# Expert pairs of a two-block decoder kernel: scatter and gather queued behind the next bias product

## The chip, the cores and the metric

One NeuronCore of one Trainium2 chip runs the whole program. The metric is the device time of one execution in microseconds, as the median of several executions of the same program. All tensors are float32, and the weights come from HBM.

## The reference, cut to what matters

The first block mixes tokens (gated delta rule and gated linear attention) and ends in a mixture of experts; the second block has two dense decoder layers with attention. The change lies in the experts alone:

```python
def moe_ffn(h, w_router, b_router, w_gu, b_gu, w_down, b_down):
    # h: 256 tokens x 1024; 32 experts, each token goes to its 4 best
    logits = h @ w_router + b_router
    top_logit, top_idx = lax.top_k(logits, 4)
    top_p = softmax(top_logit)
    # for every expert e, with the tokens that chose it (rows xb):
    gu = xb @ w_gu[e] + b_gu[e]                 # 1024 -> 2048: gate and linear half
    act = clamped_swiglu(gu)                    # sigmoid(1.702 g) * g * (l + 1), clamped at 7
    y = act @ w_down[e] + b_down[e]             # 1024 -> 1024
    # out[token] += p(token, e) * y
```

Every expert's weights are read once: 8 MB for gate and linear half, 4 MB for the way down, 12 MB for each of 32 experts (402.7 MB in all).

## The kernel before, in words

**Tiling.** `moe` keeps 64 rows for each expert (CAP) and works on two experts at a time, so that a pair fills the 128 columns of TensorE: 16 pairs, n = 0 to 15. Two pairs make a block (b = 0 to 7). Per block, a *gather* builds one-hot matrices S (VectorE, L1326) and multiplies the tokens by them (L1337: 8 feature tiles of 4 products each into a `tr` buffer), and `scaled` brings each tile to SBUF, on VectorE (L1245) and ScalarE (L1243) in turn, as `xg` (odd blocks) or in the resident `resB` (even blocks). So `xg` has two places, and the gather of the next block overwrites nothing that the current one reads.

**One pair.** (1) Gate and linear products: 8 steps kk, each with two 1 MB weight tiles, into the PSUM tiles `gt` and `lt` (L1354), closed by the bias products (L1358). (2) `swiglu`: VectorE clamps `gt` and `lt` (L1251, L1252), ScalarE does three passes (L1253 to L1255), VectorE two products (L1256, L1257). (3) `act_T`: 8 transposes (L1264) through two `tr` buffers, copied by ScalarE (L1265). (4) Way down: 4 steps f2, two 1 MB tiles each, into `yd` (L1374). (5) `scatter`: two transposes of the routing weights `sp` (L1272), a ScalarE copy to `spT` (L1274), `ys` = `yd` x gain on VectorE (L1278), and for each of 2 x 2 quarters a product with `spT` into a `tr` buffer (L1281) that VectorE adds to the residual `x1`, which is `resA` in the trace (L1282).

**Buffers.** `gt`, `lt` and `yd` have one buffer each and fill six of the eight PSUM banks. The other two are the two `tr` buffers, which the gather, the scatter, `act_T`, the bias sums and the setup of the second block all share. In SBUF, `ys` has two buffers, used in turn by `ys` itself and by ScalarE's `sg`.

**Weights.** `Experts` holds a ring of 14 tiles of 1 MB and issues every load on SyncE's queue (L1103) in the order of use. A load is issued when the ring slot that it overwrites has been read. Seventeen tiles are under way before the first pair begins.

**What sets the order.** The program is traced in Python order. The framework's scheduler then writes each engine's queue: at every point it takes the earliest traced instruction whose inputs and buffers its own plan holds to be ready. The engines run their queues strictly in order. After block 3 stands `overflow` (L1293): a branch for experts with over 64 rows, over which no instruction is moved; each engine's queue comes to it on its own. After pair 15 comes the second block, whose weights take the ring's place.

The order of tracing inside a block is plain:

```python
for b in range(8):
    S, xg = ...                        # gather of block b
    for pr in range(2):
        ...                            # gate and linear products, bias products
        swiglu(gt, lt, act)
        aT = act_T(act)
        ...                            # way down into yd
        scatter(sp, yd, squares if e0 == 30 else None)
```

Of the kernel before, what the change touches and what calls it, by code (L numbers as in the profile page):

```python
# [9 lines left out]
F32 = mybir.dt.float32  # L10
# [3 lines left out]
ALU = mybir.AluOpType  # L14
# [1114 lines left out]
CAP = 64  # L1129


def moe(k, weights, A, B):
# [132 lines left out]
            nc.scalar.copy(aT[:, 4 * q:4 * q + 4, :].rearrange("p f s -> p (f s)"), pt)  # L1265
        return aT

    def scatter(sp, yd, fn=None):

        pt = tr(256)  # L1270
        for t in range(2):
            nc.tensor.transpose(pt[:, t * 128:(t + 1) * 128], sp[:, t, :], ident)  # L1272
        spT = wk.tile([128, 256], F32, name=k.nm("spT"), tag="spT", bufs=1)
        nc.scalar.copy(spT, pt)  # L1274
        ys = wk.tile([128, 1024], F32, name=k.nm("ys"), tag="ys", bufs=2)
        for j in range(2):
            js = slice(j * 512, j * 512 + 512)
            nc.vector.tensor_mul(ys[:, js], yd[:, js], g2r[:, js])  # L1278
            for t in range(2):
                o = tr()  # L1280
                nc.tensor.matmul(o, spT[:, t * 128:(t + 1) * 128], ys[:, js], start=True, stop=True)  # L1281
                nc.vector.tensor_add(x1[:, t, js], x1[:, t, js], o)  # L1282
                if fn is not None:
                    fn(t, j)
# [6 lines left out]
    def overflow():  # L1291
        mx = nc.values_load(cnt[0:1, 32:33], min_val=0, max_val=256)
        with tc.If(mx > CAP):  # L1293
            for blk in range(2):
                lo = CAP + 128 * blk
                with tc.For_i(0, 32, 1) as e:
                    ce = nc.values_load(cnt[0:1, bass.ds(e, 1)], min_val=0, max_val=256)
                    with tc.If(ce > lo):
                        big_expert(k, L, e, lo)
            nc.vector.memset(flag, 0.0)  # L1300
        p = one.tile([128, 2, 32], F32, name="posm")
        nc.vector.tensor_scalar_add(p, pos, flag)
        return p
# [13 lines left out]
        nc.scalar.activation(jk, x1[:, t, j * 512:j * 512 + 512], AF.Square, accum_out=s4[:, t, j:j + 1])  # L1317

    iota = k.iota[:, 0:CAP]
    for b in range(8):  # L1320
        if b == 4:
            posm = overflow()
        S = []
        for t in range(2):
            s = wk.tile([128, 4, CAP], F32R, name=k.nm("S"), tag="S", bufs=4)
# [7 lines left out]
        for f in range(8):  # L1333
# [3 lines left out]
                    nc.tensor.matmul(o, hx[:, t, f * 128:(f + 1) * 128], S[t].rearrange("p e s -> p (e s)"),  # L1337
                                     start=(t == 0 and i == 0), stop=(t == 1 and i == 1))
            scaled(xg[:, f, :], o, f)
        for pr in range(2):  # L1340
            e0 = 4 * b + 2 * pr
            sp = wk.tile([128, 2, 128], F32, name=k.nm("sp"), tag="sp", bufs=2)
            for t in range(2):
                nc.vector.tensor_tensor(sp[:, t, :].rearrange("p (e s) -> p e s", e=2), S[t][:, 2 * pr:2 * pr + 2, :].bitcast(F32),
                                        prob[:, t, e0:e0 + 2].unsqueeze(2).to_broadcast([128, 2, CAP]), op=ALU.mult)
            gt = ps.tile([128, 1024], F32, name=k.nm("gt"), tag="gt", bufs=1)
            lt = ps.tile([128, 1024], F32, name=k.nm("lt"), tag="lt", bufs=1)
            quarter = lambda j: (gt, gt, lt, lt)[j][:, (j % 2) * 512:(j % 2) * 512 + 512]
            for kk in range(8):
                w = weights.two()  # L1350
                for j in range(4):
                    for i in range(2):
                        c0 = (2 * pr + i) * CAP
                        nc.tensor.matmul(quarter(j)[64 * i:64 * i + 64], xg[:, kk, c0:c0 + CAP],  # L1354
                                         w[i][:, j * 512:(j + 1) * 512], start=(kk == 0), stop=False)
            for j in range(4):
                for i in range(2):
                    nc.tensor.matmul(quarter(j)[64 * i:64 * i + 64], ident[:, 32 * j + e0 + i:32 * j + e0 + i + 1].to_broadcast([128, 64]),  # L1358
                                     bgu, start=False, stop=True)
            if e0 == 0:  # L1360
                early.__exit__(None, None, None)
                wk.late = P("mlate", reuse_waits="tile")
            if e0 == 12:
                biases(weights_T())
            act = wk.tile([128, 1024], F32, name=k.nm("act"), tag="act", bufs=1)
            swiglu(gt, lt, act)
            aT = act_T(act)
            yd = ps.tile([128, 1024], F32, name=k.nm("yd"), tag="yd", bufs=1)
            for f2 in range(4):
                w = weights.two()  # L1370
                for f in range(2):
                    for j in range(2):
                        for i in range(2):
                            nc.tensor.matmul(yd[64 * i:64 * i + 64, j * 512:(j + 1) * 512],  # L1374
                                             aT[:, 2 * f2 + f, 64 * i:64 * i + 64], w[i][:, f, j * 512:(j + 1) * 512],
                                             start=(f2 == 0 and f == 0), stop=(f2 == 3 and f == 1))
            scatter(sp, yd, squares if e0 == 30 else None)
            if e0 in (18, 22, 26):
                q = next(setup)

    s2 = one.tile([128, 2], F32, name="ms2")
    r2 = one.tile([128, 2], F32, name="mr2")
# [10 lines left out]
def big_expert(k, L, e, lo):  # L1393
# [46 lines left out]
    for f in range(8):  # L1440
        w = wk.tile([128, 1024], F32, name=k.nm("bew"), tag="ys", bufs=2)
        nc.sync.dma_start(w, w_dn[bass.ds(e, 1), f * 128:(f + 1) * 128, :].rearrange("o p d -> p (o d)"))
        for j in range(2):
            nc.tensor.matmul(yd[:, j * 512:(j + 1) * 512], aT[:, f, :], w[:, j * 512:(j + 1) * 512],
                             start=(f == 0), stop=(f == 7))
    L["scatter"](sp, yd)


def phase2_setup(k, one, tmp, psum):
# [620 lines left out]
```

## Time and profile before

| | |
|---|---|
| median of 3 executions | 2501.57 us (2495.52 to 2501.66) |
| the profiled execution's own time | 2501.63 us |
| its span, first to last instruction | 2499.9 us |
| mean granted TensorE clock | 0.958 of full |
| TensorE busy (matmuls) | 2288.2 us, 92% of the span |
| VectorE, ScalarE, GpSimdE busy | 1252.3, 929.0, 151.1 us |
| read from HBM | 602.3 MB, 241 GB/s over the span |

The expert stage lies between about 740 and 1740 us of the span. A busy TensorE is not TensorE at its peak: matmuls overlap, and each row's time includes the pipeline. In a row of a timeline the brackets at the end hold the idle time of the engine before the instruction and what ended it. Times are microseconds from the start of the span.

### The profile page before, as it was taken

Reading aid. Unit: us, or ns where it says so; the run is one execution under the profiler, and the core shown is the slowest. Engines: PE = TensorE matmul, PEld = TensorE weight load, DVE = VectorE, ACT = ScalarE, POOL = GpSimd, SP = SyncE. Lnnn points to the kernel's source line nnn. Section 1 sums busy time; section 2 is a strip of 40 time slices with the busy share of each in tenths; the row PEclk is TensorE's granted clock in tenths of the full one; section 3 lists DMA queues with packets and bytes.
Section 4 is the critical chain, followed back from the end, with each engine's and each line's share of the span. In section 5 each row is a group of like instructions: output and inputs, shape, how many; then the busy total and the mean of one; then the engine's idle time right before and its main releaser. Section 6 shows DMA issues by size and latency. Waiting matters only on the chain.

```text
span 2499.9 us, 36297 instructions
## 1 busy us (share of the span) xinstructions
PE 2288.2 (92%) x14402; PEld 1517.2 (61%) x14403; DVE 1252.3 (50%) x2676; ACT 929.0 (37%) x1956; POOL 151.1 (6%) x186
## 2 busy tenths in 40 slices
PE   6689878999989999999899999998999999999998
PEld 3476557889973333333333333333887999887998
DVE  4998887687561111112211121112867656866655
ACT  4556545577430101010001010102466555465545
POOL 0122122000010000000000000000011000011001
PEclk8799988999989999999999999999999999999999
DMA  8532331234988999999999999996534555534553
GB/s 284 139 85 55 114 112 35 60 87 117 284 304 350 407 412 401 417 404 398 387 373 415 414 413 401 407 400 230 158 105 138 175 178 159 154 111 132 189 181 109
DMA packets 290347, 605.87 MB, mean 242 GB/s; under 512 B 26038, under 2 KB 218681, under 8 KB 254332
## 3 DMA queue, kind: packets, MB, share of 16 engines
q1 hardware_dynamic: 283236, 595.24, 64.8%
q10 hardware_dynamic: 6280, 7.80, 1.2%
q8 instruction: 115, 1.88, 0.3%
q0 software_dynamic: 656, 0.46, 0.1%
q14 instruction: 60, 0.49, 0.1%
HBM read 602.30 MB, written 1.15 MB: 241 GB/s over the span
## 4 chain that ended last, share of the span: by engine, by line
PE 42%; DVE 4%; ACT 2%; issue 2%; POOL 0%; ACTq 0%; DVEq 0%; POOLq 0%
PE qm L164 22%; PE yd L1374 5%; PE gt L1354 4%; PE lt L1354 4%; PE tr L1281 1%; PE qm L1781 1%; DVE wl L151 1%; PE tr L1337 1%; PE gt L1358 0%; PE tr L1264 0%; DVE u L1587 0%; DVE act L1257 0%; DVE g L1251 0%; DVE ul L151 0%; ACT sg L1255 0%
## 5 line engine op out<-in xcount | busy, mean ns | idle before, releaser
L150 ACT CAST wh<-w 128x1024 fp32r<-128x1024 f32 (+2 forms) x318 | 318.5, 1002 | 282.6 <-PE qm L164 201.3
L151 DVE TENSOR_TENSOR wl<-w,wh 128x1024 fp32r<-128x1024 f32 (+2 forms) x318 | 372.2, 1171 | 38.9 <-ACT wh L150 37.0
L164 PE MATMUL qm<-uh,wh 128*128 128x272 f32 (+2 forms) x1008 | 260.6, 293 | 0.6 <-ACT wh L150 0.5
L1374 PE MATMUL yd<-w,aT 128*64 128x512 f32 x1024 | 260.0, 639 | 0.6 <-ACT aT L1265 0.4
L164 PE MATMUL qm<-ul,wh 128*128 128x272 f32 (+2 forms) x1008 | 257.4, 289 | 1.3 <-DVE ul L151 1.3
L1251 DVE TENSOR_SCALAR g<-gt 128x1024 f32<-128x1024 f32 x16 | 19.6, 1225 | 409.4 <-PE gt L1358 353.9
L1253 ACT ACTIVATE sg<-g 128x1024 f32<-128x1024 f32 x16 | 16.9, 1056 | 538.5 <-DVE g L1251 538.5
L164 PEld LDWEIGHTS qm<-uh,wh 128*128 128x128 f32 (+1 forms) x1008 | 188.4, 187 | 10.3 <-issue 5.8
L164 PEld LDWEIGHTS qm<-ul,wh 128*128 128x128 f32 (+1 forms) x1008 | 189.1, 188 | 3.5 <-DVE ul L151 1.9
L1354 PE MATMUL gt<-w,resB 128*64 128x512 f32 x512 | 184.0, 598 | 0.0
L1354 PE MATMUL lt<-w,resB 128*64 128x512 f32 x512 | 181.3, 593 | 0.6 <-DVE act L1252 0.6
L1354 PE MATMUL gt<-w,xg 128*64 128x512 f32 x512 | 178.3, 595 | 0.0
L1354 PE MATMUL lt<-w,xg 128*64 128x512 f32 x512 | 177.5, 593 | 0.0
L1374 PEld LDWEIGHTS yd<-w,aT 128*64 128x64 f32 x1024 | 79.0, 148 | 162.0 <-issue 153.6
L164 PE MATMUL qm<-uh,wl 128*128 128x272 f32 (+2 forms) x1008 | 144.7, 285 | 0.0
L164 PE MATMUL mm<-hTh,wh 128*128 128x256 f32 (+1 forms) x384 | 130.9, 360 | 9.6 <-ACT wh L150 4.1
L164 PEld LDWEIGHTS qm<-uh,wl 128*128 128x128 f32 (+1 forms) x1008 | 131.8, 187 | 0.5 <-issue 0.4
L164 PE MATMUL qm<-fl,wh 128*128 128x272 f32 (+1 forms) x512 | 128.5, 286 | 0.0
L164 PE MATMUL qm<-fh,wh 128*128 128x272 f32 (+1 forms) x512 | 127.3, 286 | 0.0
L164 PE MATMUL mm<-hTl,wh 128*128 128x256 f32 (+1 forms) x384 | 126.8, 349 | 0.0
L1354 PEld LDWEIGHTS lt<-w,resB 128*64 128x64 f32 x512 | 53.6, 137 | 73.0 <-issue 71.2
L1354 PEld LDWEIGHTS lt<-w,xg 128*64 128x64 f32 x512 | 53.4, 137 | 71.8 <-issue 71.4
(586 smaller groups left out, 4302.2 us busy)
## 6 DMA issues: line engine op xcount, KB each, us to landing
w<-in_w_gu_dram SPq DMA_DIRECT2D x256, 1024.0 KB
w<-in_w_down_dram SPq DMA_DIRECT2D x128, 1024.0 KB
w<-in_w_ff_dram SPq DMA_DIRECT2D x64, 1024.0 KB
w<-in_w_in_dram SPq DMA_DIRECT2D x72, 512.0 KB
w<-in_w_in_dram SPq DMA_DIRECT2D x30, 1024.0 KB
y<-in_w_mod_dram SPq DMA_DIRECT2D x19, 1024.0 KB
w<-in_w_out_dram SPq DMA_DIRECT2D x24, 512.0 KB
w<-in_w_mod_dram SPq DMA_DIRECT2D x5, 1024.0 KB
```

The lines of the kernel that those rows point to most:

```text
L150: k.nc.scalar.copy(hi, x)
L151: k.nc.vector.tensor_sub(lo, x, hi.bitcast(F32))
L164: mm = nc.tensor.matmul(out, l, r, start=start and n == 1, stop=stop and n == 3 * len(terms))
L1251: nc.vector.tensor_scalar(g, gt, 7.0, LOW / 1.702, op0=ALU.min, op1=ALU.max)
L1253: nc.scalar.activation(sg, g, AF.Exp, scale=-1.702)
L1281: nc.tensor.matmul(o, spT[:, t * 128:(t + 1) * 128], ys[:, js], start=True, stop=True)
L1337: nc.tensor.matmul(o, hx[:, t, f * 128:(f + 1) * 128], S[t].rearrange("p e s -> p (e s)"), start=(t == 0 and i == 0), stop=(t == 1 and i = ...
L1354: nc.tensor.matmul(quarter(j)[64 * i:64 * i + 64], xg[:, kk, c0:c0 + CAP], w[i][:, j * 512:(j + 1) * 512], start=(kk == 0), stop=False)
L1374: nc.tensor.matmul(yd[64 * i:64 * i + 64, j * 512:(j + 1) * 512], aT[:, 2 * f2 + f, 64 * i:64 * i + 64], w[i][:, f, j * 512:(j + 1) * 512] ...
L1781: nc.tensor.matmul(o[r, f:], v[:n, j, r], keys(ts[i], j, n)[:, f - KQ[j]:], start=(j == 0), stop=(j == 2))
```

## The change

The gather, the gate and linear products and the way down become functions, and the two loops become one over 16 pairs. `scatter` is split: `taken` (the product of `yd` with the gain, into `ys`) stays right behind a pair's way down, and the rest, with the transposes of `sp`, the products with `spT` and the sums into `x1`, is traced in the next pair, behind its `swiglu`. There the gather of the next block is traced too (after the odd pairs but 7 and 15), and in pair 6 the bias sums. All TensorE instructions of that stretch get an edge to the pair's last bias product `mm`: in TensorE's queue they come behind it, without a wait on it. Pair 7's scatter is traced ahead of the overflow branch, the gathers of blocks 0 and 4 stay ahead of their pairs, and pair 15's scatter comes after the loop. (`big_expert`, in the branch, calls both halves one after the other.)

```diff
@@ -1265,17 +1265,23 @@
             nc.scalar.copy(aT[:, 4 * q:4 * q + 4, :].rearrange("p f s -> p (f s)"), pt)
         return aT
 
-    def scatter(sp, yd, fn=None):
+    def taken(yd):
+
+        ys = wk.tile([128, 1024], F32, name=k.nm("ys"), tag="ys", bufs=2)
+        for j in range(2):
+            js = slice(j * 512, j * 512 + 512)
+            nc.vector.tensor_mul(ys[:, js], yd[:, js], g2r[:, js])
+        return ys
+
+    def scatter(sp, ys, fn=None):
 
         pt = tr(256)
         for t in range(2):
             nc.tensor.transpose(pt[:, t * 128:(t + 1) * 128], sp[:, t, :], ident)
         spT = wk.tile([128, 256], F32, name=k.nm("spT"), tag="spT", bufs=1)
         nc.scalar.copy(spT, pt)
-        ys = wk.tile([128, 1024], F32, name=k.nm("ys"), tag="ys", bufs=2)
         for j in range(2):
             js = slice(j * 512, j * 512 + 512)
-            nc.vector.tensor_mul(ys[:, js], yd[:, js], g2r[:, js])
             for t in range(2):
                 o = tr()
                 nc.tensor.matmul(o, spT[:, t * 128:(t + 1) * 128], ys[:, js], start=True, stop=True)
@@ -1317,9 +1323,9 @@
         nc.scalar.activation(jk, x1[:, t, j * 512:j * 512 + 512], AF.Square, accum_out=s4[:, t, j:j + 1])
 
     iota = k.iota[:, 0:CAP]
-    for b in range(8):
-        if b == 4:
-            posm = overflow()
+
+    def gather(b):
+
         S = []
         for t in range(2):
             s = wk.tile([128, 4, CAP], F32R, name=k.nm("S"), tag="S", bufs=4)
@@ -1337,46 +1343,70 @@
                     nc.tensor.matmul(o, hx[:, t, f * 128:(f + 1) * 128], S[t].rearrange("p e s -> p (e s)"),
                                      start=(t == 0 and i == 0), stop=(t == 1 and i == 1))
             scaled(xg[:, f, :], o, f)
-        for pr in range(2):
-            e0 = 4 * b + 2 * pr
-            sp = wk.tile([128, 2, 128], F32, name=k.nm("sp"), tag="sp", bufs=2)
-            for t in range(2):
-                nc.vector.tensor_tensor(sp[:, t, :].rearrange("p (e s) -> p e s", e=2), S[t][:, 2 * pr:2 * pr + 2, :].bitcast(F32),
-                                        prob[:, t, e0:e0 + 2].unsqueeze(2).to_broadcast([128, 2, CAP]), op=ALU.mult)
-            gt = ps.tile([128, 1024], F32, name=k.nm("gt"), tag="gt", bufs=1)
-            lt = ps.tile([128, 1024], F32, name=k.nm("lt"), tag="lt", bufs=1)
-            quarter = lambda j: (gt, gt, lt, lt)[j][:, (j % 2) * 512:(j % 2) * 512 + 512]
-            for kk in range(8):
-                w = weights.two()
-                for j in range(4):
-                    for i in range(2):
-                        c0 = (2 * pr + i) * CAP
-                        nc.tensor.matmul(quarter(j)[64 * i:64 * i + 64], xg[:, kk, c0:c0 + CAP],
-                                         w[i][:, j * 512:(j + 1) * 512], start=(kk == 0), stop=False)
+        return S, xg
+
+    def gate_up(e0, xg):
+
+        gt = ps.tile([128, 1024], F32, name=k.nm("gt"), tag="gt", bufs=1)
+        lt = ps.tile([128, 1024], F32, name=k.nm("lt"), tag="lt", bufs=1)
+        quarter = lambda j: (gt, gt, lt, lt)[j][:, (j % 2) * 512:(j % 2) * 512 + 512]
+        for kk in range(8):
+            w = weights.two()
             for j in range(4):
                 for i in range(2):
-                    nc.tensor.matmul(quarter(j)[64 * i:64 * i + 64], ident[:, 32 * j + e0 + i:32 * j + e0 + i + 1].to_broadcast([128, 64]),
-                                     bgu, start=False, stop=True)
-            if e0 == 0:
-                early.__exit__(None, None, None)
-                wk.late = P("mlate", reuse_waits="tile")
-            if e0 == 12:
+                    c0 = (e0 % 4 + i) * CAP
+                    nc.tensor.matmul(quarter(j)[64 * i:64 * i + 64], xg[:, kk, c0:c0 + CAP],
+                                     w[i][:, j * 512:(j + 1) * 512], start=(kk == 0), stop=False)
+        for j in range(4):
+            for i in range(2):
+                c = 32 * j + e0 + i
+                mm = nc.tensor.matmul(quarter(j)[64 * i:64 * i + 64], ident[:, c:c + 1].to_broadcast([128, 64]),
+                                      bgu, start=False, stop=True)
+        return gt, lt, mm
+
+    def down(aT):
+        yd = ps.tile([128, 1024], F32, name=k.nm("yd"), tag="yd", bufs=1)
+        for f2 in range(4):
+            w = weights.two()
+            for f in range(2):
+                for j in range(2):
+                    for i in range(2):
+                        nc.tensor.matmul(yd[64 * i:64 * i + 64, j * 512:(j + 1) * 512],
+                                         aT[:, 2 * f2 + f, 64 * i:64 * i + 64], w[i][:, f, j * 512:(j + 1) * 512],
+                                         start=(f2 == 0 and f == 0), stop=(f2 == 3 and f == 1))
+        return yd
+
+
+    last = None
+    for n in range(16):
+        b, e0 = n // 2, 2 * n
+        if n == 8:
+            scatter(*last)
+            last = None
+            posm = overflow()
+        if n in (0, 8):
+            S, xg = gather(b)
+        sp = wk.tile([128, 2, 128], F32, name=k.nm("sp"), tag="sp", bufs=2)
+        for t in range(2):
+            nc.vector.tensor_tensor(sp[:, t, :].rearrange("p (e s) -> p e s", e=2), S[t][:, e0 % 4:e0 % 4 + 2, :].bitcast(F32),
+                                    prob[:, t, e0:e0 + 2].unsqueeze(2).to_broadcast([128, 2, CAP]), op=ALU.mult)
+        gt, lt, mm = gate_up(e0, xg)
+        if n == 0:
+            early.__exit__(None, None, None)
+            wk.late = P("mlate", reuse_waits="tile")
+        act = wk.tile([128, 1024], F32, name=k.nm("act"), tag="act", bufs=1)
+        swiglu(gt, lt, act)
+        with tc.issue_after(mm.ins):
+            if last is not None:
+                scatter(*last)
+            if n % 2 and n not in (7, 15):
+                S, xg = gather(b + 1)
+            if n == 6:
                 biases(weights_T())
-            act = wk.tile([128, 1024], F32, name=k.nm("act"), tag="act", bufs=1)
-            swiglu(gt, lt, act)
-            aT = act_T(act)
-            yd = ps.tile([128, 1024], F32, name=k.nm("yd"), tag="yd", bufs=1)
-            for f2 in range(4):
-                w = weights.two()
-                for f in range(2):
-                    for j in range(2):
-                        for i in range(2):
-                            nc.tensor.matmul(yd[64 * i:64 * i + 64, j * 512:(j + 1) * 512],
-                                             aT[:, 2 * f2 + f, 64 * i:64 * i + 64], w[i][:, f, j * 512:(j + 1) * 512],
-                                             start=(f2 == 0 and f == 0), stop=(f2 == 3 and f == 1))
-            scatter(sp, yd, squares if e0 == 30 else None)
-            if e0 in (18, 22, 26):
-                q = next(setup)
+        last = sp, taken(down(act_T(act)))
+        if e0 in (18, 22, 26):
+            q = next(setup)
+    scatter(*last, squares)
 
     s2 = one.tile([128, 2], F32, name="ms2")
     r2 = one.tile([128, 2], F32, name="mr2")
@@ -1443,7 +1473,7 @@
         for j in range(2):
             nc.tensor.matmul(yd[:, j * 512:(j + 1) * 512], aT[:, f, :], w[:, j * 512:(j + 1) * 512],
                              start=(f == 0), stop=(f == 7))
-    L["scatter"](sp, yd)
+    L["scatter"](sp, L["taken"](yd))
 
 
 def phase2_setup(k, one, tmp, psum):
```

## Rows read from the trace of the kernel before

**Rows 1.** Page, parts 1 and 2: busy times; the DMA engines' busy share in 40 slices

```profile
PE 2288.2 (92%) x14402; PEld 1517.2 (61%) x14403; DVE 1252.3 (50%) x2676; ACT 929.0 (37%) x1956; POOL 151.1 (6%) x186
...
DMA  8532331234988999999999999996534555534553
```

**Rows 2.** Who waited for the loads (line L1103); SyncE's longest waits; TensorE's wait

```profile
  PEld gt L1354: 4.9, 16
...
SPq L1103 <- PE lt L1354: 436.9, 223, 21.5
...
PE tr L1264 <- DVE act L1257: 64.7, 16, 4.3
```

**Rows 3.** VectorE's timeline: the first clamp of pairs 1, 2 and 3

```profile
835.41 1.23 DVE L1251 TENSOR_SCALAR g<-gt 128x1024 f32<-128x1024 f32 x1 [27.78 <-PE gt L1358]
...
900.58 1.23 DVE L1251 TENSOR_SCALAR g<-gt 128x1024 f32<-128x1024 f32 x1 [27.08 <-PE gt L1358]
...
959.35 1.23 DVE L1251 TENSOR_SCALAR g<-gt 128x1024 f32<-128x1024 f32 x1 [28.64 <-PE gt L1358]
```

**Rows 4.** Timeline of pair 4 from its last bias products to the way down

```profile
1023.13 2.30 PE L1358 MATMUL lt<-bgu,cst 128*64 128x512 f32 x7
...
1027.25 1.06 ACT L1255 ACTIVATE sg<-sg 128x1024 f32<-128x1024 f32 x1
1028.34 1.23 DVE L1257 TENSOR_TENSOR act<-act,sg 128x1024 f32<-128x1024 f32 x1 [0.38 <-ACT sg L1255]
...
1029.62 1.97 PE L1264 MATMUL tr<-cst,act 128*128 128x128 f32 x8 [4.19 <-DVE act L1257]
...
1031.52 12.81 PE L1374 MATMUL yd<-w,aT 128*64 128x512 f32 x50
```

**Rows 5.** Timeline of pair 15's end: way down, scatter, second block

```profile
1730.35 0.44 PE L1272 MATMUL tr<-cst,sp 128*128 128x128 f32 x2
1730.72 3.65 PE L1374 MATMUL yd<-w,aT 128*64 128x512 f32 x14
1730.83 0.37 ACT L1274 COPY spT<-tr 128x256 f32<-128x256 f32 x1 [12.71 <-PE tr L1272]
...
1734.41 1.29 DVE L1278 TENSOR_TENSOR ys<-yd,g2r 128x512 f32<-128x512 f32 x2 [18.18 <-PE yd L1374]
1735.24 3.86 PE L1281 MATMUL tr<-ys,spT 128*128 128x512 f32 x8 [0.88 <-DVE ys L1278]
...
1738.29 0.69 DVE L1282 TENSOR_TENSOR resA<-resA,tr 128x512 f32<-128x512 f32 x1 [0.36 <-PE tr L1281]
...
1739.14 0.69 DVE L1282 TENSOR_TENSOR resA<-resA,tr 128x512 f32<-128x512 f32 x1 [0.17 <-PE tr L1281]
```

**Rows 6.** TensorE, block 1's gather of 32 products: first; last tile's first, last

```profile
864.89 0.39 PE L1337 MATMUL tr<-S,hl 128*128 128x256 f32 x1
...
872.20 0.39 PE L1337 MATMUL tr<-S,hl 128*128 128x256 f32 x1
...
872.65 0.28 PE L1337 MATMUL tr<-S,hh 128*128 128x256 f32 x1
```

**Rows 7.** Windows: busy time (instructions) of PE, PEld, DVE, ACT, POOL; clock, DMA, GB/s

```profile
788.70:792.40 3.70, 3.70 (x20) 1.25 (x18) 0.00 (x0) 0.00 (x0) 0.00 (x0) 1.00 0.00 0
...
1256.00:1500.90 244.90, 223.97 (x970) 79.86 (x968) 43.85 (x61) 23.38 (x32) 1.09 (x2) 0.97 1.01 412
...
900.00:960.00 60.00, 54.95 (x234) 18.67 (x231) 10.08 (x13) 4.71 (x6) 0.00 (x0) 0.94 1.02 416
...
792.40:1715.00 922.60, 840.35 (x3598) 301.52 (x3594) 166.09 (x231) 85.17 (x116) 1.09 (x2) 0.96 0.99 403
...
1715.00:1734.50 19.50, 17.96 (x74) 6.05 (x74) 1.32 (x2) 1.51 (x3) 0.00 (x0) 0.91 0.00 0
```

**Rows 8.** Windows of pair 2's gap and the stretch behind it

```profile
902.30:906.40 4.10, 0.00 (x0) 0.00 (x0) 3.67 (x3) 2.77 (x3) 0.00 (x0) 0.80 1.03 426
906.40:909.80 3.40, 3.36 (x12) 2.10 (x14) 0.00 (x0) 1.17 (x2) 0.00 (x0) 0.50 1.00 417
```

## The prediction

> **What bounds the kernel now.** I read the page's busy times and slices first: TensorE is busy 92% of the span, and over the expert stage (slices 14 to 27 of 62.5 us) the DMA engines are at nine tenths or more [rows 1]. Two resources near their limit: the question is which one ends last. The waits answer it. TensorE's weight loads stood 4.9 us in all for gate and linear weights, while SyncE stood 436.9 us until TensorE had read a ring slot [rows 2]. So the weights are early and TensorE sets the pace, but not by much: in the longest stretch without a pause the transfers ran at 412 GB/s, in a good 60 us at 416, over the whole stage at 403 [rows 7]. A pair's 24 loads are 25.17 MB, 61.1 us at 412 and 60.5 us at 416.
>
> What TensorE spends beside products on weights, the timelines show. Between the last bias product (it ends at 1023.13 + 2.30 = 1025.43) and the first transpose (1029.62) it is idle for 4.19 us, in which VectorE and ScalarE make the swiglu; the way down begins at 1031.52, 6.09 us after the bias products [rows 4]. These idle times sum to 64.7 us over 16 pairs [rows 2]. Then comes the scatter: 0.44 us of transposes, 0.88 us idle for `ys`, 3.86 us of products [rows 5]. And where a gather stands between two pairs, the interval from clamp to clamp is 65.17 us, where none does 58.77 us: a gather costs 6.40 us [rows 3].
>
> **What the change removes.** Fourteen of 16 scatters leave the place between two pairs (those of pairs 7 and 15 stay): 14 x (0.44 + 0.88 + 3.86) = 72.5 us. Six of 8 gathers (blocks 1, 2, 3, 5, 6, 7) leave it too: 6 x 6.40 = 38.4 us. Together 110.9 us go from where nothing covers them.
>
> **What it adds.** All of it is queued between the bias products and the transposes, where 4.19 us stand free. I count from the end of the bias products to the start of the way down, 6.09 us now.
>
> Eight gaps (pairs 2, 4, 6, 7, 10, 12, 14, 15) get a scatter alone. `spT` is ScalarE's, whose third pass ends 2.88 us into the gap [rows 4]; if the copy (0.37 us) comes behind it, the products start at 3.3. Their two `tr` buffers are the ones that the transposes need, and the third and fourth sums end 3.74 and 4.59 us after the first product [rows 5]. So the transposes start at 7.0, and with the 1.90 us from their start to the way down [rows 4] that begins at 8.9: 2.8 us later than now. If the copy slips in between the passes, nothing is added. I take 2, nearer the upper end, since the passes are traced first: 8 x 2 = 16 us.
>
> Six gaps (pairs 1, 3, 5, 9, 11, 13) get a scatter and a gather. The lower end is TensorE never waiting: 0.44 + 3.86 + 8 tiles of 0.73 (872.20 to 872.93) = 10.1 us, and 1.9 us of transposes and copy as now, 12.0, which is 5.9 more than now [rows 4 to 6]. The upper end is all in a row: the scatter's third sum to 7.0, the gather in the 8.04 us that its 8 tiles take now, paced by the two buffers (864.89 to 872.93) [rows 6], 1.9 us more: 16.9, 10.8 more than now. I take 8, as the same two buffers pace it: 6 x 8 = 48 us.
>
> TensorE's net gain is 110.9 - 16 - 48 = 47 us, between 110.9 - 22.4 - 64.8 = 24 and 110.9 - 0 - 35.4 = 76.
>
> **What else moves.** `taken` stays behind the way down; its 1.29 us were followed by TensorE's 0.88 us wait [rows 5], and now gate products follow at once; without that cover 0.88 us a pair would be back. The bias sums of pair 6 move behind its swiglu: eight VectorE passes of about 0.69 us [rows 5], 5.5 us either way, taken as nothing. The edges bind TensorE alone: VectorE's one-hot matrices may come earlier, and SyncE's queue keeps its order of loads, so no DMA moves past another. Queued behind the tied products are the transposes and the way down of the same pair, and for those SyncE waits, for ring slots: a longer gap makes the ring fuller before it empties. On VectorE the sums (0.69 us) and the even tiles stand among the swiglu's passes; that is the third rival. The clock falls to half in the stretch behind a gap (granted 0.50, the 1.2 GHz level, over 3.4 us, after 0.80 in the idle 4.1) [rows 8]; a gap with products in it may spare some of this, which I leave as a reserve of TensorE's.
>
> **Then the transfers bound it.** At 47 us less over 14 pairs TensorE would want a pair's weights in 58 to 59 us, below the 60.5 to 61.1 that they take. From the last early pause (788.7 to 792.4, the ring full) to the last landing at 1715 the queue moved 403 x 922.6 = 371.8 MB; at 412 that takes 902.4 us, at 416 893.8, so the last load lands 20.2 to 28.8 us sooner. Now nothing moves from 1715 to 1734.5 [rows 7], where the way down ends (1730.72 + 3.65 = 1734.37 [rows 5]): TensorE is 19.4 us behind its loads. A TensorE that waits for them ends one step behind, 3.65 us [rows 5]: 15.7 us more. The floor is 35.9 to 44.5 us below today. The Trainium skill's page "DMA: Bandwidth & Descriptors" (Specifications) gives about 358 GB/s of HBM for a core; by that these bytes would need 1039 us and nothing could be gained. The trace disagrees, 403 to 416, so this gets no chance.
>
> **The sum.** The smaller of 47 and about 40, less about 3 us for the early pairs, where the ring, nearly full behind the longer gaps, pauses as it does once now for 3.7 us [rows 7]: 37 us. Against the profiled execution's own 2501.63 us (span 2499.9; median 2501.57, the same) that is 2465 us.
>
> **The rivals.**
> *Under nothing.* Scatter and gather run wholly behind the swiglu and TensorE stays the bound: 24 us by the upper ends, and about 10 if each gap has one more turn of the two `tr` buffers (0.85 us from sum to sum [rows 5], 14 x 0.85 = 12): 2478 to 2490. For it: two `tr` buffers for fifteen tiles, all emptied by the two engines that make the swiglu. Against: their queues are free for most of a pair.
> *Not what it says.* The edge puts the products behind the bias products, but nothing puts them ahead of the transposes. If the plan puts them among the way down, the 4.19 us stay and only 0.88 us per scatter is saved, 12 us or less: 2489 to 2501. Against: they are traced ahead of the transposes and ready sooner.
> *Slower: the sums ahead of the product.* If VectorE's queue holds the four sums, and the gather's even tiles, ahead of the swiglu's last product (1.23 us), the product waits for TensorE, which waits for `spT`: sums end at 3.3 + 4.59 = 7.9, product at 9.1, way down at 11.0, 4.9 later than now; in gather gaps 8.04 more, 12.9 and over. 8 x 4.9 + 6 x 12.9 = 117, or 6 us slower than before, 2508; with one buffer turn more a gap, 12 us, 2520. It decides once the added time passes 110.9 us. Against: the product is traced first.
> *More from the transfers.* A 4.1 us window shows 426 GB/s [rows 8]; at that the floor falls to 65 us and TensorE's 47 count: 2454. The Trainium skill's table has a fabric ceiling of 435 GB/s (same page and section), by which the floor would lie 84 us below; no stretch of this trace reaches it.
>
> **Chances and range.** Forecast (2457 to 2470): 0.55. Under nothing: 0.25. Not what it says: 0.08. Slower: 0.07. More from the transfers: 0.05. The range 2454 to 2490 holds the first, nearly all of the second and the last, and leaves out some 15 in 100. No change is what this kernel's runs can't tell, 0.3%: 2494 to 2509. Faster: 0.55 + 0.25 + 0.05 and a part of the second rival, 0.87; same 0.06; slower 0.07.
>
> **What would show it.** Right: scatter and gather products between bias products and transposes; gate products directly behind the way down; clamp to clamp near 60.5 to 61 us in even and odd pairs alike in the later half; waits of TensorE's weight loads for DMA well above 4.9 us; the way down of pair 15 ending within 5 us of the last landing, near 1697. Wrong: SyncE still waiting mostly for TensorE and a TensorE that never waits for weights (first rival), an idle gap of 4 us as before (second), or the swiglu's last product much later than 2.9 us after the bias products (third).

## The result and the profile after

The changed kernel took 2473.2 us (median of 4 executions, 2471.81 to 2475.28) against 2501.61 us (4 executions, 2495.52 to 2505.29) of the kernel before beside it: a ratio of 0.9889, with an interval of 0.9868 to 0.9911. Forecast were 2465 us, in a range of 2454 to 2490. The profiled execution took 2471.81 us with a span of 2470.0, so 29.9 us less span than before, where the forecast had 37.

The page first: the lines that answer to [rows 1], what the transfers moved in each of 40 slices, and the engines' shares of the chain that ended last:

```profile
PE 2284.5 (92%) x14402; PEld 1546.0 (63%) x14403; DVE 1243.4 (50%) x2676; ACT 925.4 (37%) x1956; POOL 151.0 (6%) x186
...
DMA  8522431134898999999999999996524555534563
GB/s 286 142 77 52 120 120 35 45 94 121 254 329 325 416 416 416 416 416 416 388 415 415 416 415 416 416 416 237 157 84 151 179 175 160 153 103 140 188 187 104
...
PE 35%; DMA 9%; DVE 4%; issue 2%; ACT 1%; POOL 0%; ACTq 0%; SPq 0%; DVEq 0%; POOLq 0%
```

TensorE is busy the same 92%: from that line alone nobody would see that the bound has moved. The slices of 61.8 us show it: 415 to 416 GB/s in every slice of the expert stage but the one of the overflow branch (388). The chain that ended last now runs through transfers for 9% of the span; in the profile of before it held none.

The stretches, as in [rows 7] (busy time of PE, PEld, DVE, ACT, POOL, then clock, DMA share, GB/s), from the last early pause to the last landing, the later half, and the stretch behind the last landing:

```profile
790.00:1692.00 902.00, 845.13 (x3632) 331.09 (x3630) 159.27 (x232) 82.92 (x118) 1.09 (x2) 0.99 1.01 412
1256.00:1677.00 421.00, 394.23 (x1704) 154.28 (x1701) 67.70 (x97) 37.81 (x53) 1.09 (x2) 0.99 1.02 416
...
1692.00:1701.80 9.80, 9.77 (x42) 2.95 (x38) 0.00 (x0) 0.37 (x1) 0.00 (x0) 1.00 0.00 0
```

The transfers hold 416 GB/s over 421 us, the most that any long stretch of these traces shows; the 426 of the short window of [rows 8] did not come back. The last load lands at 1692 instead of 1715, and the stretch in which nothing moves before the way down ends is 10 us instead of 19.5.

Who waits for whom has turned round too. SyncE's waits at the loads' line, and what waited for the loads, as in [rows 2] (us in total, times, longest):

```profile
SPq L1103 <- DMA w<-in_w_gu_dram: 210.4, 117, 3.5
SPq L1103 <- PE lt L1358: 177.8, 104, 16.9
...
SPq L1103 <- PE yd L1374: 144.7, 41, 16.5
...
SPq L1103 <- DMA w<-in_w_down_dram: 93.9, 56, 2.2
```
```profile
  PEld gt L1358: 41.9, 52
...
  PE gt L1358: 14.1, 21
```

TensorE's weight loads waited 41.9 us for weights where they had waited 4.9 us, and SyncE waited for TensorE's gate products 177.8 us where it had been 436.9.

VectorE's first clamps of pairs 11 to 14, as in [rows 3]:

```profile
1434.16 1.23 DVE L1251 TENSOR_SCALAR g<-gt 128x1024 f32<-128x1024 f32 x1 [37.35 <-PE gt L1363]
...
1494.74 1.23 DVE L1251 TENSOR_SCALAR g<-gt 128x1024 f32<-128x1024 f32 x1 [1.43 <-PE gt L1363]
...
1555.21 1.22 DVE L1251 TENSOR_SCALAR g<-gt 128x1024 f32<-128x1024 f32 x1 [36.00 <-PE gt L1363]
...
1615.59 1.23 DVE L1251 TENSOR_SCALAR g<-gt 128x1024 f32<-128x1024 f32 x1 [30.29 <-PE gt L1363]
```

60.6, 60.5, 60.4 us: a pair with a gather in its gap and one without take the same, as long as 25.17 MB take at 416 GB/s (60.5 us; the pairs just before and behind these took 61.8). Before they took 65.2 and 58.8 in turn [rows 3].

The gap of pair 2 holds a scatter alone (timeline from the last bias products to the way down, as in [rows 4]):

```profile
886.03 1.94 PE L1363 MATMUL lt<-bgu,cst 128*64 128x512 f32 x8
...
887.89 0.44 PE L1280 MATMUL tr<-cst,sp 128*128 128x128 f32 x2
...
888.51 0.35 ACT L1282 COPY spT<-tr 128x256 f32<-128x256 f32 x1
888.76 1.06 ACT L1254 ACTIVATE sg<-sg 128x1024 f32<-128x1024 f32 x1
...
888.91 1.98 PE L1287 MATMUL tr<-ys,spT 128*128 128x512 f32 x4 [0.58 <-ACT spT L1282]
...
890.48 0.68 DVE L1288 TENSOR_TENSOR resA<-resA,tr 128x512 f32<-128x512 f32 x1
891.07 1.22 DVE L1257 TENSOR_TENSOR act<-act,sg 128x1024 f32<-128x1024 f32 x1
...
891.21 1.13 PE L1287 MATMUL tr<-ys,spT 128*128 128x512 f32 x2 [0.31 <-DVE resA L1288]
...
892.94 1.12 PE L1287 MATMUL tr<-ys,spT 128*128 128x512 f32 x2 [0.61 <-DVE resA L1288]
...
895.43 13.95 PE L1374 MATMUL yd<-w,aT 128*64 128x512 f32 x64
```

The scatter is where the change wanted it. ScalarE copies `spT` between two of its passes, and VectorE takes one sum ahead of the swiglu's last product, which ends at 892.29, 4.3 us after the bias products (887.97). In the gap that held 4.19 us of nothing TensorE now waits in pieces of 0.3 to 0.6 us. The gap is 895.43 - 887.97 = 7.46 us. The gap of pair 1, with a gather, runs from 830.01 to 843.06: 13.05 us.

TensorE at the end of pair 15 (timeline, as in [rows 5]; its wait for the last gate weights, the last bias products, the way down):

```profile
1671.97 1.50 PE L1358 MATMUL gt<-w,xg 128*64 128x512 f32 x5 [2.00 <-DMA w<-in_w_gu_dram]
...
1676.80 2.25 PE L1363 MATMUL lt<-bgu,cst 128*64 128x512 f32 x5
...
1686.45 11.37 PE L1374 MATMUL yd<-w,aT 128*64 128x512 f32 x50
...
1698.12 3.65 PE L1374 MATMUL yd<-w,aT 128*64 128x512 f32 x14
```

The way down ends at 1701.77, 32.6 us earlier than in [rows 5] (1734.37). What stands behind it takes 768.3 us of the span, before it took 765.5: 2.8 us go there, so 29.9 are left.

### The profile page after: what moved, and what is told of

The parts are those of the page before. It is cut to its first block, busy times and chain, and to the rows that moved or that the text cites. A ratio compares the mean times of both kernels' runs of the same rounds, so it can differ in the third digit from the quotient of the medians.

```text
span 2470.0 us, 36281 instructions
## 1 busy us (share of the span) xinstructions
PE 2284.5 (92%) x14402; PEld 1546.0 (63%) x14403; DVE 1243.4 (50%) x2676; ACT 925.4 (37%) x1956; POOL 151.0 (6%) x186
## 4 chain that ended last, share of the span: by engine, by line
PE 35%; DMA 9%; DVE 4%; issue 2%; ACT 1%; POOL 0%; ACTq 0%; SPq 0%; DVEq 0%; POOLq 0%
PE qm L164 23%; DMA w<-in_w_gu_dram 6%; PE yd L1374 2%; DMA w<-in_w_down_dram 2%; PE gt L1358 2%; PE lt L1358 2%; PE qm L1811 1%; DVE wl L151 1%; PE tr L1343 1%; DVE u L1617 0%; PE tr L1287 0%; PE qp L1878 0%; ACT wh L150 0%; PE lt L1363 0%; PE qp L1823 0%
## 5 line engine op out<-in xcount | busy, mean ns | idle before, releaser
L1374 PE MATMUL yd<-w,aT 128*64 128x512 f32 x1024 | 228.4, 600 | 0.2 <-ACT aT L1265 0.2
L1358 PE MATMUL lt<-w,resB 128*64 128x512 f32 x512 | 189.5, 594 | 0.6 <-DVE act L1252 0.6
L1358 PE MATMUL lt<-w,xg 128*64 128x512 f32 x512 | 188.4, 597 | 0.0
L1374 PEld LDWEIGHTS yd<-w,aT 128*64 128x64 f32 x1024 | 72.9, 138 | 143.3 <-issue 140.3
L1273 DVE TENSOR_TENSOR ys<-yd,g2r 128x512 f32<-128x512 f32 x32 | 20.6, 686 | 248.1 <-PE yd L1374 231.4
L1358 PEld LDWEIGHTS lt<-w,xg 128*64 128x64 f32 x512 | 60.4, 138 | 71.4 <-issue 69.3
```

## The experiments

My theory was that the transfers now bound the stage, that scatter and gather each have more cover than is needed, and that the end of pair 15 holds what the forecast missed. The main rivals were that TensorE still sets the pace, and that the edge does nothing. In all diffs the file compared with is the changed kernel, unless said. Kernels that ran on one chip share the runs of the kernel before; a ratio is always to that kernel.

### The same kernel again

No edit.

> The changed kernel once more, beside the parts taken singly. Both theories: 2471 to 2476 us; in its profile the last weight tile lands near 1692 us and the way down of pair 15 ends some 10 us later.

2471.58 us, ratio 0.9882 (0.986 to 0.9903). Beside the last experiment below it was run once more.

> The changed kernel beside the two, for comparison: 2471 to 2476, lag 10.

2469.08 us, ratio 0.9875 (0.9852 to 0.9897). With the first result that makes gains of 28, 30 and 31 us.

### One part alone

Scatters moved, gathers ahead of their pairs as before:

```diff
-        if n in (0, 8):
+        if n % 2 == 0:
             S, xg = gather(b)
...
-            if n % 2 and n not in (7, 15):
-                S, xg = gather(b + 1)
...
```

> Only the scatters are moved; every gather stays ahead of its block. Theory (the transfers bound the stage): TensorE gains 14 x 5.18 less about 14 x 1.4 for longer gaps, 53 us, more than the transfers allow, so the time is within 5 us of the whole change: 2473 to 2479. Rival (TensorE is still the bound and the parts add up): 72.5 of the 110.9 us removed, 18 to 19 us of the 28: 2482 to 2484.

Gathers moved, scatters directly behind the way down as before:

```diff
-            scatter(*last)
-            last = None
...
-            if last is not None:
-                scatter(*last)
...
-        last = sp, taken(down(act_T(act)))
+        scatter(sp, taken(down(act_T(act))), squares if n == 15 else None)
...
-    scatter(*last, squares)
```

> Only the gathers are moved; every scatter stays behind its way down. Theory: TensorE stays the bound: six gaps hold a gather of about 6.2 us in place of 4.2 idle us, 2 to 2.5 us longer each, so 38.4 - 14 = 24 us off: 2474 to 2482, with the loads waiting for ring slots as before. Rival (parts add up in proportion to what is removed): 10 us off: 2491.

2471.53 us, ratio 0.9884 (0.9862 to 0.9906), and 2470.52 us, ratio 0.9874 (0.9857 to 0.989). Either half of the change gives all of it. Both times lie a little below what the theory expected (2473 to 2479 and 2474 to 2482) and well below the rival's sums. Who waited for the loads, first with the scatters alone, then with the gathers alone:

```profile
  PEld gt L1358: 36.1, 42
  PE gt L1358: 13.4, 16
```
```profile
  PEld gt L1358: 4.8, 8
```

With the scatters alone TensorE starves much as with both. With the gathers alone it hardly does (4.8 us), and yet nothing is lost: its own pace is then just under that of the transfers, and the ring lends the difference. Three first clamps of that kernel, pairs 1 to 3:

```profile
831.85 1.23 DVE L1251 TENSOR_SCALAR g<-gt 128x1024 f32<-128x1024 f32 x1 [27.78 <-PE gt L1363]
...
890.88 1.22 DVE L1251 TENSOR_SCALAR g<-gt 128x1024 f32<-128x1024 f32 x1 [28.64 <-PE gt L1363]
...
949.47 1.23 DVE L1251 TENSOR_SCALAR g<-gt 128x1024 f32<-128x1024 f32 x1 [28.64 <-PE gt L1363]
```

59.0 and 58.6 us against the transfers' 60.5. The two pairs of [rows 3] took 62.0 us on average, 1.5 above the 60.5. Either half of the change takes more than that off TensorE's part, so the other half has nothing left to buy.

### Half of the way down's bytes

In both kernels each step of the way down loads one tile, and both experts use it, so a pair loads 20 MB instead of 24 with the same instructions on TensorE:

```diff
-        self.order = [(d, p, kk, i) for p in range(16) for d, n in ((0, 8), (1, 4)) for kk in range(n) for i in range(2)]
+        self.order = [(d, p, kk, i) for p in range(16) for d, n in ((0, 8), (1, 4)) for kk in range(n) for i in range(2 - d)]
...
+    def one(self):
...
+        w = self.have.pop(t)
+        return w, w
...
-            w = weights.two()
+            w = weights.one()
```

> The changed kernel with half of the way-down weights left out: both experts of a pair use the first one's tile, 20 loads a pair in place of 24 (64 MB less); TensorE does the same work. Theory (the transfers bound the changed kernel): TensorE's own pace shows, about 58 us for a pair with a gather in its gap and 52.6 for one without, so the stage ends some 55 to 65 us sooner: 2408 to 2420. Rival (TensorE and its hand-overs are the bound): within 6 us of 2473.

> The kernel before with the same loads left out (half of the way-down weights, each pair's second tile replaced by its first). Theory (TensorE set its pace, the transfers only just kept up): 0 to 6 us faster than before, 2495 to 2502. Rival (the transfers held it back already): 10 us or more faster.

The changed kernel fell to 2417.13 us, ratio 0.9668 (0.964 to 0.9696), within the theory's figure: what held it was bytes. Its first clamps (pairs 1 to 3) show TensorE's own pace:

```profile
822.13 1.22 DVE L1259 TENSOR_SCALAR g<-gt 128x1024 f32<-128x1024 f32 x1 [23.58 <-PE gt L1371]
...
880.41 1.23 DVE L1259 TENSOR_SCALAR g<-gt 128x1024 f32<-128x1024 f32 x1 [25.31 <-PE gt L1371]
...
932.78 1.22 DVE L1259 TENSOR_SCALAR g<-gt 128x1024 f32<-128x1024 f32 x1 [27.94 <-PE gt L1371]
```

58.3 us with a gather in the gap, 52.4 without: 6.9 and 6.4 us less than in [rows 3]. From the first clamp to the end of pair 15's way down it takes 871.6 us, where the kernel before takes 955.1 (779.3 to 1734.4): 83.5 us less.

The kernel before fell to 2487.55 us, ratio 0.9944 (0.9931 to 0.9957), 13 us faster where the theory had 0 to 6: a miss, of the rival's size. But bytes explain little of it: TensorE's weight loads waited 7.4 us in all for weights in the trace of before, and 4.3 in this one. TensorE's waits at the scatter's products are a better explanation. In the trace of before, then in that of the half-loads version of it (the only row there for these products):

```profile
PE tr L1281 <- DVE ys L1278: 12.2, 14, 0.9
```
```profile
PE tr L1289 <- ACT spT L1282: 4.2, 8, 0.5
```

With fewer loads the framework planned another order, in which gate products stand ahead of the scatter's and cover the wait: 8.0 of the 13.2 us. Another 5.1 us lie in the first interval from clamp to clamp (51.06 us against 56.12): there the new order fills pair 0's gap with 18 records of the next pair's gate products, where the kernel before has 4. The run shows that such an edit also changes the order. So it is no clean test of the bytes, but the changed kernel fell by some 54 us (ratio 0.9668 against 0.9882), far more than the 13 of the kernel before.

### No scatter at all

The 14 moved scatters are left out, so `x1` lacks these experts' part.

```diff
-            if last is not None:
-                scatter(*last)
```

> The changed kernel without the scatters of 14 of the 16 pairs (their sums are left out; all loads stay). Theory (the transfers are the bound): only the last gap counts, 1 to 4 us faster: 2469 to 2472. Rival (TensorE's gaps are the bound): 14 x 4 us or more faster, below 2425.

2474.98 us, ratio 0.9899 (0.9871 to 0.9928). From the first clamp (781.3) to the end of the way down (1705.27) it takes 924.0 us; the changed kernel takes 923.8 (778.0 to 1701.77). Fourteen scatters cost no time where they are now. The profiled execution took 6 us more than that of the changed kernel: its stage started 3.2 us later, and what stands behind the way down took 2.6 us more, neither of which I can explain. The 1 to 4 us that were expected from the last gap did not come: with that gap empty, nothing moves for the last 10.3 us before the way down ends (1695.0 to 1705.3), as in the changed kernel.

### No edge

```diff
-        with tc.issue_after(mm.ins):
+        if True:
```

> The order of tracing is the new one, but the TensorE instructions are not tied behind the last bias product. Theory (the edge does the work): the scatter's products fall back among the way down and the next gate products, the idle 4.2 us of every gap stay: 2494 to 2503. Rival (tracing order is enough): as the whole change, 2471 to 2476.

2525.39 us, ratio 1.009 (1.0073 to 1.0107): 24 us slower than the kernel before, and outside both figures. The gap was left empty, as expected without the edge, and the scatter and the gather were put among the next pair's gate products. TensorE in pair 2's gap, and behind it (timeline):

```profile
909.92 1.97 PE L1264 MATMUL tr<-cst,act 128*128 128x128 f32 x8 [4.19 <-DVE act L1257]
```
```profile
931.84 1.50 PE L1358 MATMUL gt<-w,xg 128*64 128x512 f32 x5
...
935.42 1.98 PE L1287 MATMUL tr<-ys,spT 128*128 128x512 f32 x4
937.33 1.07 PE L1358 MATMUL gt<-w,xg 128*64 128x512 f32 x2
938.24 1.02 PE L1358 MATMUL lt<-w,xg 128*64 128x512 f32 x2
939.19 0.39 PE L1343 MATMUL tr<-S,hl 128*128 128x256 f32 x1
```

No time is idle in the second stretch, and yet it is slow. A product of the queue shows as two records. From 937.33 to 939.19 there are two products, in the queue both of the same expert, that is of the same 64 columns: 1.86 us, 0.93 each. From 931.84 to 935.42 there are six, four of one expert and two of the other: 3.58 us, four times 0.90. A step of eight in the changed kernel, four of each, takes 3.44 us (eight records of each half, 0.43 us apart), four times 0.86. So two products on the two halves of the columns run side by side, and a stretch between two full-width products costs what its busier half costs. I counted that over the queue: between full-width products, one half has more products than the other by 116 in all in this kernel, by 52 in the kernel before and by 12 in the changed one. Two products left without a partner take 0.86 us more than two side by side, so the 64 more than before are some 27 us (an estimate). The windows of before and of this kernel, from the first clamp to the end of the way down:

```profile
779.30:1734.40 955.10, 869.03 (x3710) 311.52 (x3706) 172.21 (x236) 91.03 (x124) 1.09 (x2) 0.96 0.96 393
```
```profile
784.10:1762.70 978.60, 905.33 (x3710) 348.26 (x3706) 170.91 (x236) 90.61 (x124) 1.09 (x2) 0.95 0.95 383
```

The stage lost 23.5 us: TensorE is busy 36.3 us longer with the same products, of which the products without a partner explain 27, and it is idle 12.8 us less. That leaves some 9 us of busy time without a cause.

### The order of the halves alone

To see whether the two halves must stand next to each other in the queue, I exchanged the two loops of the gate products, so that four products of one expert stand ahead of four of the other:

```diff
-            for j in range(4):
-                for i in range(2):
+            for i in range(2):
+                for j in range(4):
```

> The changed kernel with the loops over the gate products' quarters and the pair's two experts exchanged: of each chunk all products of one expert's 64 columns are queued first, then all of the other's, so that no product stands beside one of the other column half. Theory (two products that use the two halves of the columns run side by side only where they stand next to each other in TensorE's queue; four products took 0.91 us so paired in the changed kernel and 1.86 us where a foreign product parted them in no_edge): the gate products of a pair go from some 27 us to some 55 us, TensorE bounds the stage instead of the transfers, and 16 x 27.4 = 439 us less the slack that TensorE had (some 5 us a pair) gives about 2800 to 2870 us. Rival (the order of the halves does not matter, and what no_edge lost is only the waits that stand among the gate products): 2469 to 2476 us.

2477.91 us where the kernel before took 2509.26 beside it, one execution each: 31 us less, as for the changed kernel. The time that the theory expected was missed by over 300 us. TensorE's timeline from the first gate products of a pair:

```profile
918.59 1.88 PE L1358 MATMUL gt<-w,xg 128*64 128x512 f32 x4
920.31 0.59 PE L1358 MATMUL lt<-w,xg 128*64 128x512 f32 x1
920.31 0.64 PE L1358 MATMUL gt<-w,xg 128*64 128x512 f32 x1
920.74 0.59 PE L1358 MATMUL lt<-w,xg 128*64 128x512 f32 x1
920.79 0.59 PE L1358 MATMUL gt<-w,xg 128*64 128x512 f32 x1
```

The first two products of the first expert (four records of `gt`) run alone for 1.72 us. Then two records start every 0.43 us, one of each expert: a product of `lt` of the first beside one of `gt` of the second, which stands two places behind it in the queue. So it goes on through the pair: in most pairs the first 1.72 us are single, the rest is side by side. The halves need not be neighbours, but the reach is short: products two places apart overlapped, and the second expert's first product, four places behind the first one's, did not start with it. The sentence ahead of the prediction that the engines run their queues strictly in order is thus not quite right for TensorE: the second expert's `gt` starts ahead of the first expert's last `lt`. What is lost, 1.72 us a pair, doesn't show in the time, since the transfers bound it.

What parts the halves in the version without the edge is then the full-width product: in its trace the runs of half-width products between full-width ones are those of the queue, so none was started across one. The Trainium skill's page "TensorEngine Tiling (Array Packing)" (Key Properties) says that tiles work independently of each other, and that a change of the tiling mode drains TensorE. The traces agree with the second (1.86 us for two products of one half between two full-width ones), and with the first within that reach. The other version of the theory, that only neighbours overlap, was mine and is wrong.

### The bias products ahead of the gate products

The edge hangs on the last product of the pair, so with the bias products first fewer products stand behind the last load:

```diff
+        for j in range(4):
+            for i in range(2):
+                c = 32 * j + e0 + i
+                nc.tensor.matmul(quarter(j)[64 * i:64 * i + 64], ident[:, c:c + 1].to_broadcast([128, 64]),
+                                 bgu, start=True, stop=False)
         for kk in range(8):
...
-                    nc.tensor.matmul(quarter(j)[64 * i:64 * i + 64], xg[:, kk, c0:c0 + CAP],
-                                     w[i][:, j * 512:(j + 1) * 512], start=(kk == 0), stop=False)
-        for j in range(4):
-            for i in range(2):
-                c = 32 * j + e0 + i
-                mm = nc.tensor.matmul(quarter(j)[64 * i:64 * i + 64], ident[:, c:c + 1].to_broadcast([128, 64]),
-                                      bgu, start=False, stop=True)
+                    mm = nc.tensor.matmul(quarter(j)[64 * i:64 * i + 64], xg[:, kk, c0:c0 + CAP],
+                                          w[i][:, j * 512:(j + 1) * 512], start=False, stop=(kk == 7))
```

> The changed kernel with the bias products of each pair ahead of its weight products instead of behind them; the tied work then follows the last weight product. Theory (the transfers set the landing of the last weights, and what stands behind them sets the end: the last gate step, 3.65 us of bias products, the gap, the way down): the last landing moves by 0 to 3 us, the way down ends about 6 us behind it instead of 10, 2465 to 2470 us. Rival (the lag is the ring's, the order inside a pair does not matter): as the changed kernel, 2471 to 2476, lag 10.

The second version also takes pair 14's scatter out of pair 15's gap and puts it behind that pair's bias products, ahead of its gate products (`mm` is then their last one):

```diff
+        if e0 == 30:
+            with tc.issue_after(mm.ins):
+                scatter(*last)
...
-            if last is not None:
+            if last is not None and n < 15:
                 scatter(*last)
```

> The same, and pair 15's gap without a scatter: pair 14's scatter comes behind pair 15's bias products, ahead of its weights. Theory: 1 to 2 us less lag again, about 5 us, 2464 to 2469. Rival: no further change.

2468.0 us, ratio 0.9866 (0.9844 to 0.9887), and 2464.88 us, ratio 0.9862 (0.9839 to 0.9885), beside 2469.08 us of the changed kernel on the same chip. The intervals overlap widely, so neither can be told from it. The traces show what each did. From the last landing to the end of the way down it is 6.59 us (1697.07 to 1703.66) and 6.99 us (1687.93 to 1694.92), where the changed kernel has 9.87. The first takes off 3.3 us, about as much as the bias products last, as the theory said. The second gives nothing more, where the theory had another 1 to 2 us: the end of pair 15 there, and the clock behind its gap:

```profile
1675.91 1.97 PE L1264 MATMUL tr<-cst,act 128*128 128x128 f32 x8 [4.12 <-DVE act L1257]
1677.81 9.72 PE L1377 MATMUL yd<-w,aT 128*64 128x512 f32 x34
```
```profile
1675.90:1679.30 3.40, 3.39 (x12) 2.10 (x14) 0.00 (x0) 1.17 (x2) 0.00 (x0) 0.50 1.03 413
```

With the scatter gone the gap stands empty for 4.12 us, TensorE comes out of it at half clock (granted 0.50, the 1.2 GHz level, over 3.4 us), and the first 34 records of the way down take 9.72 us; in the first version, with the scatter in the gap, they took 7.94.

## Why the prediction was right, and where it was not

**The forecast's case came.** The transfers bound the stage, as the waits, the equal pairs of 60.5 us and the half-loads run show. The last load landed 23.1 us sooner; 20.2 to 28.8 were forecast. The time came out 8 us above the forecast, within its range.

**The step that failed: "A TensorE that waits for them ends one step behind, 3.65 us".** It ended 9.9 us behind (1691.9 to 1701.8), which took 6.2 of the 37 us. TensorE's last wait is not in the way down. It is at the last gate weights, 1671.97; behind these stand the step and the bias products (to 1679.05), the gap (7.4) and the way down (15.3), 29.8 us in all, while the 8 loads of the way down land within 20 us. So the loads get ahead again during pair 15's gap, and the way down runs at TensorE's pace to the end. This could have been known beforehand: some 30 us of TensorE's against eight tiles at 2.52 us. I had followed the transfers to their end and not asked where the last wait would stand. The two runs with the bias products first take 3.3 and 2.9 us off this stretch alone.

**Right in kind, off in size: TensorE's gain of 47 us.** The scatter gap read above costs 1.4 us and not 2, as the copy did slip in between ScalarE's passes; the gather gap 7.0 and not 8. By the prediction's own sum that is 110.9 - 11 - 42 = 58. But the half-loads run shows 83.5 us over the stage (69.6 against the half-loads version of before, whose order differs). The rest is in part what I had left as a reserve, the clock. The way down of pair 4 took 16.8 us with the scatter's two transposes in it (1031.52 to 1047.69 + 0.59); behind a gap with products in it, and whole, it takes 13.95, at full clock:

```profile
895.40:909.40 14.00, 14.00 (x67) 4.83 (x68) 0.00 (x0) 0.59 (x1) 0.00 (x0) 1.00 1.02 421
```

Less the 0.44 us of the transposes, which are in the 72.5 already, that is 2.4 us for each of 14 pairs, 34 us. The clock is 1.4 of the 2.4: pair 15's way down stands behind a full gap but still has two transposes in it, and took 15.3 us. The other 1.0 was not in the prediction: full-width transposes in the way down part the column halves (see "No edge"), and the change took them out of 13 of the 16. 58 and 34 make 92, 8.5 too many. Some 6 of these are the bias sums, which were taken as nothing: in the half-loads run pair 6's gap makes its interval 62.3 us, where others without a gather have 52.4, and before they made theirs 68.9, where others with a gather had about 65. None of this changed the time, as the transfers took over long before.

**The early pairs.** 3 us were set aside for a ring that fills, and were not needed. The pause from 787.6 to 789.8 is 2.2 us where it was 3.7, and ends 2.6 us sooner; from there to the last landing it is 902.1 us at 412 GB/s, as in the lower case of the forecast (902.4). Pairs 0 to 2 ran at 50.3 to 58.0 us, TensorE's pace.

**The rest of the difference.** Behind the way down the rest of the span took 768.2 to 768.3 us in the three profiles of this kernel, 765.5 in that of before, and between 766.2 and 770.9 in those of the other kernels. I have no cause for it, and no experiment was made on it. So the 29.9 us are 23.1 for the last landing and 9.5 for the stretch from there to the end of the way down (15.7 forecast), less these 2.8.

**The rivals.** Under nothing: TensorE does wait for weights, so no. Not what it says: the edge does it, and without it the plan puts the products among the gate products, not in the way down, at a cost that I had not seen: 24 us lost, where this rival had up to 12 saved. The sums ahead of the product: one of four stands there, and the product ends 4.3 us after the bias products instead of 4.1. More from the transfers: 416 GB/s was all. The Trainium skill's page "DMA: Bandwidth & Descriptors" (Specifications) has about 358 GB/s for a core, half of what the row gives for the memory that two cores share; this one core alone moved 416 over 421 us.

## What to carry to other kernels

Where two resources lie within a few per cent of each other, a change that frees one is worth only the distance to the other: here 84 us of TensorE's time bought 30, and half of the change would have bought the same. At the end of such a stage, look for the last wait and add up what stands behind it on the engine, since the loads may all have landed long before. A gap with useful work in it was worth more than the work, because TensorE came out of it at full clock and not at half (1.4 us a gap here); and where halves of the columns are used as two, keep full-width products out of the run, or put them where both halves have had equally many.

## What the runs showed that was not expected

- A product over all 128 columns parts the two column halves: between two of them, two products of one half took 1.86 us and six, four to two, 3.58 us, with no idle time shown. Inside a run without such a product, products of the two halves ran side by side when they stood two places apart in the queue; at four places the first half ran alone for 1.72 us.
- An edge that only fixes an order, without a wait, was worth 54 us (2525.39 against 2471.58 beside it), nearly twice the gain of the change.
- Taking a scatter out of a gap made the work behind the gap slower: 34 records of the way down took 9.72 us behind an empty gap and 7.94 us behind a full one.
